# First layer's products at 164 columns, its gathered rows in four token sets, and the second layer's first gate computed in its own mixing

## The chip, the cores and the metric

The kernel runs on one core of one Trainium2 chip. The time is the device's, in microseconds, for one execution; the numbers below are medians of executions, and one further execution was profiled. TensorE (PE in the profile, its weight loads PEld) multiplies, VectorE (DVE) and ScalarE (ACT) work on elements, GpSimd (POOL) issues the indirect gathers, and SyncE (SP) issues most of the other transfers. The core has 16 DMA engines, which all queues share.

## The reference

One sequence of 256 tokens with 1024 features goes through two layers. Each layer is modulated by a conditioning vector `c`: six vectors of 1024 (shift, scale and gate for each of two halves) come out of one product with `w_ada`.

```python
def hybrid_layer(x, c_act, ...):
    mod = (c_act @ w_ada + b_ada)[:, None, :]
    sh1, sc1, g1, sh2, sc2, g2 = jnp.split(mod, 6, axis=-1)
    h = rms_norm(x, norm1_g) * (1 + sc1) + sh1
    proj = h @ w_in                       # attention, short convolution, spatial gating
    ...
    x = x + g1 * (merged @ w_out)
    h2 = rms_norm(x, norm2_g) * (1 + sc2) + sh2
    x = x + g2 * peer_ffn(h2, ...)

def peer_ffn(h, w_pq, sub_keys, expert_down, expert_up):
    # per token: 8 heads, each picks 16 of 128*128 experts by product keys
    ...
    u = expert_down[experts]              # 128 rows of 1024 for a token
    act = gelu(einsum('td,thkd->thk', t, u))
    wgt = gate * act
    vv = expert_up[experts]
    return einsum('thk,thkd->td', wgt, vv)
```

All is float32.

## The kernel before, in words

A layer has three stages. **Mixing**: 16 chunks of `w_in`, attention, convolution and gating, then 8 chunks of `w_out`. **Retrieval**: 16 chunks of `w_pq`, scores and the top-16 picks. **Experts**, by far the longest: the 16384 experts are taken in two ways at once.

- `T = DENSE[layer]` tokens (168 in the first layer, 160 in the second) are treated densely: all 16384 down vectors are multiplied with these tokens (128 chunks of 128 experts, 8 products each, `chunk_mm`, line 387; "down"), gelu and the gates are applied, and all up vectors are multiplied with the result (128 chunks, `add`, line 1201; "up"). The gates come as one-hot products for four tokens at a time (`compare`, `factors`, `gate_mm`, `gate_use`: VectorE, ScalarE, TensorE, then both again); there are `NG = T // 4` such groups.
- The other `TS = 256 - T` tokens (88 and 96) are treated by rows: for each of them GpSimd gathers the 128 down rows that it picked, one to a partition (`fetch`, line 1104), VectorE multiplies them with the token and sums (`dot`, line 1114); in up it gathers the 128 up rows, and VectorE adds them with their weights (`add_row`, line 1129 and, for the first of a set, 1127). These tokens are packed in sets of 64, 32, 16 or 8 (`token_sets`); each set has its copy of the tokens' inputs and its sum in one place of the tile `spots` (`R_DX`, `R_SUM`). At the end TensorE folds the sums of all sets into the result (`folds`, line 1207).

In `experts` the code of both halves stands in one order written by hand (`manual_schedule`), and each engine works through its instructions in that order. `dot` calls are spread over the chunks of down by a rate, `DOT_RATE`, per chunk; `add_row` calls evenly over chunks 4 to 124 of up. A row that has been used frees its buffer, and `fetch` issues the next gather. Buffers are places in the `arena` that are free at that time.

Weights are streamed in the order of the list `seq`, which the code builds for both layers. A chunk of kind "whole", "second" or "mat" goes through the ring `raw`, five units of two chunks; a "mat" chunk is then split in a high and a low part (`hi`, `lo`, three buffers each; ScalarE at line 297 or 299, VectorE at 290 or 292), so that TensorE can use three quicker products. Kind "ada" is a chunk of `w_ada`, and VectorE multiplies it with the activated `c` and sums (`ada_chunk`, line 243). Kind "aside" is the same for the next layer, loaded in the experts stage into the buffers of `hi` and `lo`, which are not used there, and worked off by `run_aside`, one at a time, in VectorE's order. `ASIDES_AT[layer]` says at which chunks of down the asides stand; the rest is spread over up. SyncE's queue takes these loads in order, and waits where a buffer is not free.

The first layer's experts carry 40 asides: the vectors 0 to 4 of the second layer. The second layer's experts carry 8 (vector 5).

## Time and profile before

| | |
|---|---|
| median of 3 runs | 1566.23 us (1564.98 to 1573.41) |
| profiled execution | 1569.29 us, span 1567.3 us |
| mean granted clock of TensorE | 0.991 |
| HBM read | 564.02 MB |
| first layer: down, up | about 190 to 513 us, 513 to 813 us |
| second layer: mixing and retrieval, down, up | 816 to 972 us, 972 to 1281 us, 1281 to 1560 us |

The page of the profile gives busy times of the engines, the span in 40 slices, the DMA queues, the chain of work that ended last, and groups of instructions with what ended the idle time before them (`<-`). A window is a stretch of the span, counted from its start. `x` is a count of instructions. TensorE handles one float32 product as two instructions, and in a busy stretch a matmul's recorded time overlaps the next one's, so the distance between them counts, not their length.

### The profile page before, as it was taken

The numbers are of one execution on the slowest core, as the hardware profiler recorded it, in microseconds if no ns is written. First come the engines' busy times: TensorE is split into PE (matmuls) and PEld (weight loads), VectorE is DVE, ScalarE is ACT, GpSimd is POOL, SyncE is SP. The second block draws the span as 40 slices with busy tenths as digits, with TensorE's granted clock in tenths as the row PEclk, the third lists the DMA queues.
The fourth block names the chain that finished last, engine by engine and source line by source line (L and its number), as shares of the span: only waits on it lengthen the run. The fifth ranks groups of instructions, "written<-read, shape, count | busy, mean of one in ns | idle before, by whom it ended". The sixth has DMA issues, their size and how long they took to land.

```text
span 1567.3 us, 28461 instructions
## 1 busy us (share of the span) xinstructions
PE 1537.3 (98%) x11240; PEld 1502.3 (96%) x11240; DVE 1000.1 (64%) x2255; ACT 475.9 (30%) x1356; POOL 496.1 (32%) x424
## 2 busy tenths in 40 slices
PE   7999999999999999999999999999999999999998
PEld 5879999999999999999999899999999999999998
DVE  6787897677787445544336678977777764444434
ACT  2346321465564000000025763224565620000000
POOL 1000133433443433434300001245354345445441
PEclk9999999999999999999999999999999999999999
DMA  9998289999999999999964562899999999999995
GB/s 385 366 383 296 98 318 339 419 422 421 422 420 415 418 423 422 423 424 422 424 243 161 188 245 97 322 350 423 423 423 421 419 420 423 423 423 422 423 424 245
DMA packets 121829, 571.16 MB, mean 364 GB/s; under 512 B 14259, under 2 KB 14787, under 8 KB 89568
## 3 DMA queue, kind: packets, MB, share of 16 engines
q1 hardware_dynamic: 48528, 241.06, 39.0%
q0 software_dynamic: 55744, 202.36, 32.2%
q10 hardware_dynamic: 17424, 125.93, 19.4%
q8 instruction: 88, 1.44, 0.3%
q14 instruction: 45, 0.37, 0.1%
HBM read 564.02 MB, written 4.09 MB: 362 GB/s over the span
## 4 chain that ended last, share of the span: by engine, by line
PE 80%; DMA 8%; issue 5%; POOL 3%; DVE 2%; ACT 1%; SPq 0%; POOLq 0%; DVEq 0%; ACTq 0%
PE acc L1201 37%; PE ch L387 26%; DMA arena<-in_down_rows,arena 6%; PE ch L389 2%; POOL arena L1104 2%; PE ch L390 2%; PE ch L391 2%; PE g L1163 1%; DMA raw<-in_w_ada 1%; PE ch L476 1%; PE acc L391 1%; PE g L982 1%; PE acc L389 1%; PE acc L390 1%; PE acc L387 1%
## 5 line engine op out<-in xcount | busy, mean ns | idle before, releaser
L1201 PE MATMUL acc<-arena,raw 128*128 128x168 f32 (+1 forms) x4096 | 575.3, 303 | 3.1 <-issue 3.1
L1201 PEld LDWEIGHTS acc<-arena,raw 128*128 128x128 f32 x4096 | 573.3, 191 | 3.5 <-issue 3.5
L387 PE MATMUL ch<-arena,raw 128*128 128x168 f32 (+2 forms) x3808 | 568.2, 308 | 1.6 <-issue 1.6
L387 PEld LDWEIGHTS ch<-arena,raw 128*128 128x128 f32 x3808 | 542.6, 191 | 8.0 <-issue 4.3
L1129 DVE SCALAR_TENSOR_TENSOR spots<-arena,spots 128x1024 f32<-128x1024 f32 x156 | 200.4, 1284 | 194.9 <-DMA arena<-in_up_rows,arena 193.6
L1104 POOL DMA_INDIRECT arena<-in_up_rows,arena x159 | 211.8, 1332 | 291.6 <-DMA arena<-in_up_rows,arena 172.0
L1104 POOL DMA_INDIRECT arena<-in_down_rows,arena x151 | 181.0, 1199 | 228.7 <-DVE arena L1114 169.9
L1114 DVE SCALAR_TENSOR_TENSOR arena<-arena,spots 128x1024 f32<-128x1024 f32 x151 | 182.9, 1222 | 59.9 <-DMA arena<-in_down_rows,arena 59.5
L243 DVE SCALAR_TENSOR_TENSOR aside<-aside,arena 128x1024 f32<-128x1024 f32 x48 | 58.6, 1221 | 69.2 <-DMA aside<-in_w_ada 69.2
L1147 ACT ACTIVATE arena<-arena,parts 128x128 f16<-128x128 f16 x164 | 64.6, 394 | 122.1 <-DVE arena L1137 102.7
L418 ACT ACT_TABLE_LOAD x6 | 7.7, 1283 | 275.5 <-PE acc L1201 275.4
L387 PE MATMUL ch<-arena 128*128 128x160 f32 (+2 forms) x512 | 81.5, 318 | 3.7 <-issue 1.9
L389 PE MATMUL ch<-hh,hi 128*128 128x256 f32 x288 | 82.6, 288 | 2.0 <-DVE arena L507 1.9
L387 PEld LDWEIGHTS ch<-arena 128*128 128x128 f32 x512 | 75.7, 193 | 8.4 <-ACT arena L440 4.1
L1180 ACT ACTIVATE arena<-ch 128x336 f32<-128x336 f32 (+32 forms) x122 | 42.2, 346 | 130.5 <-PE ch L387 101.7
L390 PE MATMUL ch<-hh,lo 128*128 128x256 f32 x288 | 81.8, 284 | 0.0
L391 PE MATMUL ch<-hh,hi 128*128 128x256 f32 x288 | 81.7, 284 | 0.0
L290 DVE TENSOR_TENSOR lo<-raw,hi 128x1024 fp32r<-128x1024 f32 x42 | 51.4, 1230 | 26.7 <-ACT hi L297 26.6
L1173 DVE SCALAR_TENSOR_TENSOR arena<-arena,g 128x336 f32<-128x336 f32 (+30 forms) x82 | 40.3, 492 | 43.9 <-ACT arena L1171 40.5
L243 DVE SCALAR_TENSOR_TENSOR raw<-raw,arena 128x1024 f32<-128x1024 f32 x48 | 58.4, 1225 | 8.6 <-DMA raw<-in_w_ada 5.1
L1151 ACT ACTIVATE arena<-arena,parts 128x128 f16<-128x128 f16 x164 | 63.4, 386 | 0.0
L1149 ACT ACTIVATE arena<-arena,parts 128x128 f16<-128x128 f16 x164 | 63.4, 386 | 0.0
(231 smaller groups left out, 1694.9 us busy)
## 6 DMA issues: line engine op xcount, KB each, us to landing
raw<-in_up SPq DMA_DIRECT2D x64, 1024.0 KB
raw<-in_up ACTq DMA_DIRECT2D x64, 1024.0 KB
raw<-in_down SPq DMA_DIRECT2D x58, 1024.0 KB
raw<-in_down ACTq DMA_DIRECT2D x56, 1024.0 KB
raw<-in_w_ada SPq DMA_DIRECT2D x48, 512.0 KB
aside<-in_w_ada SPq DMA_DIRECT2D x48, 512.0 KB
raw<-in_w_pq SPq DMA_DIRECT2D x32, 512.0 KB
arena<-in_down SPq DMA_DIRECT2D x28, 512.0 KB
```

What stands on the lines that cost most here:

```text
L243: nc.vector.scalar_tensor_tensor(raw, raw, 1.0, cact, op0=OP.mult, op1=OP.mult, accum_out=mods[layer][:, col:col + 1])
L387: nc.tensor.matmul(dst, hi[:, cols], k[0], start=start, stop=stop, **kw)
L389: nc.tensor.matmul(dst, hi[:, cols], k[0], start=start, stop=False, **kw)
L390: nc.tensor.matmul(dst, lo[:, cols], k[0], start=False, stop=False, **kw)
L391: nc.tensor.matmul(dst, hi[:, cols], k[1], start=False, stop=stop, **kw)
L1104: nc.gpsimd.indirect_dma_start(out=held[n], out_offset=None, in_=rows if n >= TS else down_rows[:, :], in_offset=bass.IndirectOffsetOnAxis ...
L1114: nc.vector.scalar_tensor_tensor(row, row, 1.0, R_DX[which(k)[0]], op0=OP.mult, op1=OP.mult, accum_out=R_DOTS[:, k:k + 1])
L1129: nc.vector.scalar_tensor_tensor(R_SUM[s], row, w, R_SUM[s], op0=OP.mult, op1=OP.add)
L1147: nc.scalar.activation(og[0][:, 0, i, :], oh[:, 0, i, :], AF.Copy, scale=parts[:, 0, t + i:t + i + 1])
L1149: nc.scalar.activation(og[1][:, 0, i, :], oh[:, 0, i, :], AF.Copy, scale=parts[:, 1, t + i:t + i + 1])
L1151: nc.scalar.activation(og[0][:, 1, i, :], oh[:, 1, i, :], AF.Copy, scale=parts[:, 0, t + 2 + i:t + 3 + i])
L1201: nc.tensor.matmul(acc[d // 2][:, (d % 2) * S:(d % 2) * S + T], u[:, d * P:(d + 1) * P], acts[:, i, :], start=i == 0 and d % 2 == 0, stop= ...
```

## The change

The dense part of the first layer goes from 168 to 164 tokens. Its rows are then 92, which need four sets (64, 16, 8, 4), so `token_sets` learns the size 4, all four places of `spots` hold sets, and the staging row `R_DROW` moves to a free place of the arena. `DOT_RATE` of the first layer goes from 0.85 to 0.88. Vector 2 of the second layer (`g1`, the gate of its first half) leaves the asides, 40 of which become 32, and its eight chunks are mixed as kind "ada" into the second layer's own list, between chunks 4 and 20 of `w_in` and `w_out`. The asides of both layers stand elsewhere. And two buffers, one of `hi` and one of `lo`, become row buffers for the length of `experts`.

```diff
-DENSE = (168, 160)
+DENSE = (164, 160)
...
-DOT_RATE = (0.85, 0.92)
+DOT_RATE = (0.88, 0.92)
...
-ASIDES_AT = ((20,) * 6 + tuple(range(46, 125, 5)), (20,) * 6 + (60, 72))
+ASIDES_AT = ((20,) * 4 + tuple(range(46, 116, 5)), (20,) * 4 + (50, 60, 70, 80))
 ASIDES_UP = (4, 100)
+MIXED = (4, 20)
...
 def token_sets(n):
-    for m in (64, 32, 16, 8):
+    for m in (64, 32, 16, 8, 4):
...
-    assert off == n and len(out) <= 3
+    assert off == n and len(out) <= 4
...
-        body += mix(tail[:6], ada(0, [5])) + tail[6:] if layer == 0 else tail
+        body = body + mix(tail[:6], ada(0, [5])) + tail[6:] if layer == 0 else mix(body + tail, ada(1, [2]), *MIXED)
...
-        aside = ada(1, [0, 1, 2, 3, 4] if layer + 1 < DEPTH else [5], "aside")
+        aside = ada(1, [0, 1, 3, 4] if layer + 1 < DEPTH else [5], "aside")
...
-        R_DROW = spots[:, 3, :]
         beyond = [region(at * S, D) for at in (80, 84) if at * S >= P * T]
+        R_DROW = spots[:, 3, :] if len(SETS) < 4 else beyond.pop()
         passing = []
-        free = deque([spots[:, n, :] for n in range(len(SETS), 3)] + [region(108 * S, D)] + beyond)
+        spare_rows = [stream.tile([P, D], F32, name="row", tag=tag, bufs=3) for tag in ("hi", "lo")]
+        free = deque([spots[:, n, :] for n in range(len(SETS), 3)] + [region(108 * S, D)] + beyond + spare_rows)
```

## The prediction

> **What bounds the kernel now.** I read the page's busy line and its GB/s row first, then the DMA issues, then stage by stage the windows, the chain of waits and single engines' timelines.

> ```profile
> span 1567.3 us, 28461 instructions
> ...
> PE 1537.3 (98%) x11240; PEld 1502.3 (96%) x11240; DVE 1000.1 (64%) x2255; ACT 475.9 (30%) x1356; POOL 496.1 (32%) x424
> ...
> GB/s 385 366 383 296 98 318 339 419 422 421 422 420 415 418 423 422 423 424 422 424 243 161 188 245 97 322 350 423 423 423 421 419 420 423 423 423 422 423 424 245
> ...
> aside<-in_w_ada SPq DMA_DIRECT2D x48, 512.0 KB
> ...
> spots<-dot_in POOLq DMA_DIRECT2D x3, 512.0 KB
> ```

> PE is busy for 98% of the span, which says TensorE. But the GB/s row is flat near 421 through both layers' expert stages (slices 8 to 20 belong to the first layer). Two resources are full at once, and the question is which of them has room left when the first layer ends. The windows of that layer (length, then busy time of PE, PEld, DVE, ACT, POOL, then granted clock, DMA share, GB/s):

> ```profile
> 235.00:255.00 20.00, 20.00 (x130) 20.00 (x130) 19.56 (x73) 3.67 (x7) 10.59 (x11) 0.91 0.92 268
> 255.00:275.00 20.00, 20.00 (x143) 20.00 (x142) 10.41 (x25) 4.11 (x10) 4.58 (x5) 1.00 1.02 416
> ...
> 285.00:513.00 228.00, 227.63 (x1770) 224.06 (x1769) 164.73 (x317) 126.62 (x449) 89.05 (x75) 1.00 1.02 420
> 513.00:660.00 147.00, 143.92 (x988) 143.47 (x987) 74.57 (x73) 0.29 (x1) 59.97 (x50) 0.98 1.02 421
> 660.00:790.00 130.00, 130.00 (x915) 130.00 (x914) 54.74 (x53) 1.28 (x1) 44.40 (x34) 1.00 1.02 423
> 790.00:800.00 10.00, 10.00 (x73) 10.00 (x72) 3.92 (x4) 0.29 (x1) 0.00 (x0) 1.00 0.82 293
> ```

> From 255 to 790 us the DMA moves 416 to 423 GB/s in these windows (268 before): it is full for 535 us, while PE is full too. Who gives way? In the second half of the layer ("up", 513 to 813) it is VectorE, in the groups of instructions of that stretch; the timelines of VectorE, TensorE and the SP queue at its end show by how much:

> ```profile
> L1129 DVE SCALAR_TENSOR_TENSOR spots<-arena,spots 128x1024 f32<-128x1024 f32 x76 | 97.6, 1284 | 73.2 <-DMA arena<-in_up_rows,arena 72.2
> ...
> 796.42 1.28 DVE L1129 SCALAR_TENSOR_TENSOR spots<-arena,spots 128x1024 f32<-128x1024 f32 x1 [1.16 <-DMA arena<-in_up_rows,arena]
> ...
> 810.09 0.73 PE L1207 MATMUL acc<-fold,spots 128*128 128x64 f32 x6
> ...
> 792.90 34.36 SPq L229 DMA_DIRECT2D raw<-in_w_in  x14
> ```

> VectorE stands 73.2 us before row additions, 72.2 of it for the rows' gathers. The last row is added at 797.7 us, and it still waited 1.16 us for its gather. TensorE needs the sums first in its folds (L1207), at 810.1 us. So the DMA side has 12.4 us of room at the end of the first layer, and this is all of it. The next layer's weights (in_w_in) start at 792.9, when the rows are nearly through.

> **The change part by part.**

> *Products 164 wide.* Per chunk eight products, each recorded as two instructions, so 32 instructions for a pair of chunks. The chain of waits in the first layer and in the second, which is already 160 wide:

> ```profile
> 430.08 4.62 PE ch L387 x32
> 434.70 0.46 PE g L1163 x8
> 435.16 4.61 PE ch L387 x32
> ...
> 1139.04 4.40 PE ch L387 x32
> 1143.44 0.46 PE g L1163 x8
> 1143.90 4.40 PE ch L387 x32
> ```

> A pair takes 5.08 us with its gate at 168 columns and 4.86 at 160: 0.22 us for eight columns, 0.11 for four. Times 64 pairs that is 7.0 us in each of the two halves, 14.0 us. One gate group of four tokens fewer (42 to 41): 0.46 us. TensorE would so be 14.5 us earlier at the fold: 795.6 us.

> *Four more row tokens, eight fewer side weights.* A row gather and a side weight (aside) are both 128x1024 f32, 512 KB, one block of 0.524 MB; at 421 GB/s a block costs 1.245 us of DMA. Each half gets four row gathers more (88 to 92) and four asides fewer (22 to 18 in down, 18 to 14 in up): no change in bytes. But the time in which they must move is shorter. In the steady part of down a pair needs two weight chunks, 2 x 0.85 rows and 0.4 asides, 4.10 blocks or 5.10 us, against a pair of 5.08: in balance. Afterwards it is 2 + 1.76 + 0.4 = 4.16 blocks, 5.18 us, against 4.97 on TensorE. Chunks 46 to 111 are 32 pairs: rows come up to 6.8 us late there. VectorE takes its work in order, so the gates' factors queue behind a late row's dot product, and TensorE waits for them. Two further row buffers (one, net, in this layer, since the fourth set takes a place) hold rows; they do not move bytes. I expect 0 to 6.8 us of waits in down, say 3; it won't matter for the sum, because of what comes next.

> The two buffers come out of the tags hi and lo, which the asides use: they have four places in place of six. An aside without a place holds the SP queue, and half of the chunks' weights stand behind it there. From the waits of the SP queue:

> ```profile
> SPq L229 <- DVE aside L243: 25.9, 4, 12.9
> ```

> Up to 12.9 us, four times, and TensorE did not wait. As asides in the list fall by as much (four at chunk 20 for four places), I cost it at nothing; without that cover it is one such wait less what the weights are ahead, at most 12.9 us.

> *The end of the first layer.* What must land before the last row: one copy more of the inputs for the fourth set (the dot_in issues go from 3 to 4), one block; two asides fewer loaded ahead of 255 us (the list starts with four at chunk 20, was six), two blocks that move into the full stretch; less one block for the added buffer. Net two blocks, 2.5 us. And next-layer weights: they follow TensorE's release of buffers, 14 issues in 34.36 us, so 7 in the 17.2 us from 792.9 to the fold. With TensorE ahead, those 7 blocks start ahead of the last rows and share the DMA: 8.7 us. Against it the window 790 to 800 had 128 GB/s unused, up to 3 us. Bounds: the last addition at 797.7 (nothing pushed) to 809 (all pushed); nearest is all pushed, as the queue is full to the end: 807 us. TensorE, ready at 795.6 or a little later, waits some 11 us at its fold for what it won. The fold starts 3 us earlier than before, not 14.5.

> *Folds of a fourth set.* 8 column blocks, two instructions each, 16 more. The chain has:

> ```profile
> 813.12 3.45 PE acc L1207 x30
> ```

> 0.115 us each, 1.8 us on the path. *The clock after the wait.* A stop of TensorE has a price, seen where up begins:

> ```profile
> 522.00:528.00 6.00, 2.92 (x15) 2.47 (x14) 4.13 (x5) 0.00 (x0) 3.00 (x5) 0.82 1.03 425
> 528.00:534.00 6.00, 6.00 (x28) 6.00 (x27) 0.00 (x0) 0.00 (x0) 1.68 (x2) 0.61 1.04 429
> ```

> 3.1 us idle, then granted clocks of 0.82 and 0.61 over 12 us: 3.4 us of work lost. At the fold I take 2.5, between nothing and 3.4, since VectorE's updates take part of the path there. [...]

> Down and up of the first layer together: -3 + 1.8 + 2.5 = +1.3 us.

> *Second layer's first gate in its own mixing.* Eight weights of 512 KB now come in the main ring on SP, between chunks 5 and 19 of that layer, each followed on VectorE by one multiply-and-sum, and one addition at the end. Prices and places:

> ```profile
> L243 DVE SCALAR_TENSOR_TENSOR raw<-raw,arena 128x1024 f32<-128x1024 f32 x48 | 58.4, 1225 | 8.6 <-DMA raw<-in_w_ada 5.1 <-ACT arena L445 3.5
> ...
> 107.00:114.00 7.00, 5.28 (x33) 4.44 (x31) 4.30 (x8) 3.43 (x6) 0.00 (x0) 0.92 0.99 380
> 114.00:121.00 7.00, 5.98 (x32) 5.98 (x33) 5.17 (x9) 1.28 (x2) 0.00 (x0) 0.59 1.02 419
> 850.00:874.00 24.00, 24.00 (x193) 22.99 (x192) 21.25 (x55) 17.56 (x52) 0.00 (x0) 1.00 0.49 161
> 874.00:890.00 16.00, 16.00 (x114) 11.64 (x113) 6.98 (x12) 10.46 (x19) 0.61 (x1) 1.00 0.26 90
> ```

> The DMA has room there (161 and 90 GB/s). VectorE: 8 x 1.225 = 9.8 us in some 70; from 874 on it is idle for half the time, but from 850 to 874 it has 2.75 us free and would get three or four of the eight, 3.7 to 4.9 us. What queues behind are the low halves of the weights and the softmax steps, for which TensorE waits. Bounds: 0 (all in gaps) to 9.8. The nearest row is the first layer's output stage, which already carries eight such weights: TensorE idle 1.72 + 1.02 us from 107 to 121, with its DMA full, which here it isn't. I take 2.

> *Second layer's experts.* Asides at chunks 20 (four) and 50 to 80, instead of six and two; two more row buffers. A pair needs 2 + 1.84 blocks, 4.78 us, of 4.86: enough for two asides over 40 pairs. 0, between -2 and +2.

> Sum: +1.3 + 2 + 0 = +3.3 us. The profiled execution took 1569.29 us (span 1567.3), 3.06 above the median of 1566.23; on the median the sum gives 1569.5.

> **Rivals.** *A, the DMA does not end last.* For it: TensorE has never waited for weights (98% busy), and the rows' margin of 12.4 us is close to the 14.5 us that TensorE gains; if the rows end by 796, the whole gain stays: 1566.2 - 14.5 + 1.8 + 2 = 1555.5. It needs 11 us of DMA time from somewhere, and no window shows more than 429 GB/s in 6 us or 423 in 130. [...] The trace bears 421.

> *B, slower: VectorE in the second layer's mixing.* One place, 850 to 874 us: if the eight multiply-and-sums delay the low halves one for one, TensorE loses up to 9.8 us: 1566.2 + 1.3 + 9.8 = 1577.3. It decides once the weights' lead over TensorE is used up, that is when more than 2.75 us land in that window. For it: VectorE at 89% there. Against it: its 56% free right behind.

> *C, the layer ends as before.* The forecast is in part this: the columns saved do not show, as the rows' bytes set the end. How far it is complete is the 797.7 to 809 above.

> **How the numbers follow.** What can be told from no change is about 0.5%, 7.8 us. Forecast with C: 0.56, 1564 to 1576 (rows' end 803 to 812, mixing 0 to 5). A: 0.22, 1550 to 1561. B: 0.22, 1575 to 1584. Faster than 1558.4: A's share, 0.22; slower than 1574: B and the forecast's upper edge, 0.24; same 0.54. The range leaves out A's lower part and B's upper part, a tenth each: 1555 to 1579.

> **What would show it.** Right: pairs 4.97 us apart in down where nothing waits; the GB/s row still flat, and longer, to the layer's end; a wait of TensorE of about 10 us at L1207 or at the products before it, released by L1129; in_w_in issues ahead of the last row addition; the layer's end within 4 us of 816.6 (813.12 + 3.45); eight L243 instructions among L290 in the mixing. Wrong: no wait at L1207 and the layer ended by 806 (A), or idle TensorE in the mixing, released by L290, L517 or L721, of over 5 us (B). A wait of TensorE in down of more than 7 us would show the gates queued behind late rows to be worse than I have it.

## The result, and the profile after

The changed kernel took 1584.97 us in the median of five runs (1584.09 to 1586.43), the kernel before 1566.23 (now 1563.33 to 1573.41 in five): a ratio of 1.0113, 95% interval 1.0092 to 1.0134. It is slower, by more than the range (up to 1579) allowed for. Of the changed kernel's page, the busy line, the GB/s row and the costliest row of VectorE:

```profile
span 1584.7 us, 28490 instructions
...
PE 1533.9 (97%) x11248; PEld 1495.4 (94%) x11248; DVE 1005.7 (63%) x2267; ACT 471.4 (30%) x1347; POOL 526.2 (33%) x435
...
GB/s 385 360 388 298 102 300 353 422 422 422 421 421 410 422 423 422 423 424 422 422 175 204 218 244 96 303 342 411 423 421 422 421 422 424 423 423 422 423 424 232
...
L1131 DVE SCALAR_TENSOR_TENSOR spots<-arena,spots 128x1024 f32<-128x1024 f32 x137 | 176.1, 1286 | 228.5 <-DMA arena<-in_up_rows,arena 226.8
```

TensorE is busy for 3.4 us less (1537.3 before), and the span is 17.4 us longer: time went into stops, not into work. The GB/s row stands near 422 from slice 8 to slice 20 (410 in slice 13), as it did before; that the DMA is full for longer shows in the window from 790 to 800 us below, with 420 GB/s where the kernel before had 293. (L1131 is the row addition, L1129 before.) Where the stages begin in the two traces, in us, and how much longer each one became:

| stage | before | after | change | forecast |
|---|---|---|---|---|
| first layer's down | 190.1 to 512.6 | 189.8 to 514.0 | +1.7 | -4.5 |
| its up, to the first fold | to 810.1 | to 798.6 | -12.8 | -7.0 |
| first fold to the second layer's start | to 816.4 | to 824.5 | +19.6 | +12.8 |
| second layer's mixing | to 914.7 | to 927.8 | +5.0 | +2 |
| retrieval | to 971.3 | to 984.4 | 0 | 0 |
| second layer's down | to 1280.6 | to 1297.9 | +4.3 | 0 |
| up and the end | to 1567.3 | to 1584.7 | +0.1 | 0 |

(Forecast: 7.0 us for each half, 0.46 for the gate group and 3 of waits in down; the third row is what its +1.3 leaves. The first row starts 0.3 us earlier in the changed kernel.) Up gained more than its 7.0, as the stop at 522 to 534 us is gone. The windows of the changed kernel's first layer, columns as in the forecast's windows:

```profile
285.00:513.00 228.00, 222.29 (x1722) 215.29 (x1721) 163.04 (x313) 122.99 (x438) 91.33 (x77) 0.99 1.02 419
513.00:660.00 147.00, 146.66 (x1055) 146.55 (x1054) 68.43 (x64) 0.44 (x1) 61.48 (x47) 1.00 1.02 423
660.00:790.00 130.00, 130.00 (x936) 130.00 (x935) 53.46 (x51) 1.58 (x2) 52.96 (x38) 1.00 1.02 423
790.00:800.00 10.00, 9.15 (x68) 9.05 (x66) 5.26 (x4) 2.09 (x2) 2.13 (x4) 1.00 1.03 420
800.00:810.00 10.00, 0.59 (x2) 0.50 (x2) 5.45 (x5) 0.20 (x1) 0.00 (x0) 0.57 0.56 229
810.00:825.00 15.00, 14.51 (x65) 14.51 (x66) 6.83 (x14) 4.30 (x11) 0.00 (x0) 0.50 0.20 71
```

In down TensorE is now idle for 5.7 us of 228. From 800 to 810 it does nothing, as the forecast has it. But then it does its folds for 14.5 us at a granted clock of 0.50. The timelines of TensorE and of VectorE at that place:

```profile
798.64 0.51 PE L1209 MATMUL acc<-fold,spots 128*128 128x64 f32 x4
801.64 0.59 PE L1209 MATMUL acc<-fold,spots 128*128 128x8 f32 x2 [2.49 <-DVE spots L1131]
810.49 0.59 PE L1209 MATMUL acc<-fold,spots 128*128 128x4 f32 x2 [8.26 <-DVE qg L566]
...
816.14 8.53 PE L1209 MATMUL acc<-fold,spots 128*128 128x64 f32 x40
```

```profile
807.83 1.28 DVE L1131 SCALAR_TENSOR_TENSOR spots<-row,arena,spots 128x1024 f32<-128x1024 f32 x1 [1.25 <-DMA row<-in_up_rows,arena]
809.15 1.28 DVE L1131 SCALAR_TENSOR_TENSOR spots<-arena,spots 128x1024 f32<-128x1024 f32 x1
810.35 0.15 DVE L566 TENSOR_SCALAR qg<-vec 128x1 f32<-128x1 f32 x1
```

The fold needs the fourth set last, and the last addition ends at 810.4. (The 8.26 us are put down to L566, the small instruction that follows it on VectorE.) The 40 fold instructions at the end take 0.21 us each; in the kernel before a fold instruction took 0.115. The trace's record of the granted clock has it at half (a granted clock of 0.50) from 801.3 us for 27.3 us without a break.

### The profile page after: what moved, and what is told of

It reads as the page before. It is cut to its first block, busy times and chain, and to the rows that moved or that the text cites. A ratio compares the mean times of both kernels' runs of the same rounds, so it can differ in the third digit from the quotient of the medians.

```text
span 1584.7 us, 28490 instructions
## 1 busy us (share of the span) xinstructions
PE 1533.9 (97%) x11248; PEld 1495.4 (94%) x11248; DVE 1005.7 (63%) x2267; ACT 471.4 (30%) x1347; POOL 526.2 (33%) x435
## 3 DMA queue, kind: packets, MB, share of 16 engines
HBM read 568.74 MB, written 4.11 MB: 361 GB/s over the span
## 4 chain that ended last, share of the span: by engine, by line
PE 49%; DMA 32%; issue 7%; DVE 6%; POOL 4%; ACT 2%; SPq 0%; POOLq 0%; ACTq 0%; DVEq 0%
PE acc L1203 18%; PE ch L388 17%; DMA arena<-in_up_rows,arena 15%; DMA arena<-in_down_rows,arena 7%; DMA row<-in_up_rows,arena 3%; POOL arena L1106 3%; DMA raw<-in_w_ada 2%; PE ch L390 1%; PE ch L391 1%; PE ch L392 1%; DMA row<-in_down_rows,arena 1%; DMA spots<-in_down_rows,arena 1%; PE ch L477 1%; PE g L1165 1%; PE acc L392 1%
## 5 line engine op out<-in xcount | busy, mean ns | idle before, releaser
L1203 PE MATMUL acc<-arena,raw 128*128 128x164 f32 (+1 forms) x4096 | 566.3, 301 | 0.3 <-issue 0.3
L388 PE MATMUL ch<-arena,raw 128*128 128x164 f32 (+2 forms) x3808 | 561.5, 306 | 5.1 <-ACT arena L1185 3.5
L1131 DVE SCALAR_TENSOR_TENSOR spots<-arena,spots 128x1024 f32<-128x1024 f32 x137 | 176.1, 1286 | 228.5 <-DMA arena<-in_up_rows,arena 226.8
L1116 DVE SCALAR_TENSOR_TENSOR arena<-arena,spots 128x1024 f32<-128x1024 f32 x129 | 156.4, 1222 | 68.0 <-DMA arena<-in_down_rows,arena 67.7
L1149 ACT ACTIVATE arena<-arena,parts 128x128 f16<-128x128 f16 x162 | 63.8, 394 | 138.4 <-DVE arena L1139 130.8
L1182 ACT ACTIVATE arena<-ch 128x320 f32<-128x320 f32 (+40 forms) x122 | 41.8, 342 | 125.2 <-PE ch L388 101.9
L244 DVE SCALAR_TENSOR_TENSOR raw<-raw,arena 128x1024 f32<-128x1024 f32 x56 | 67.7, 1216 | 14.3 <-DMA raw<-in_w_ada 10.5
L1131 DVE SCALAR_TENSOR_TENSOR spots<-row,arena,spots 128x1024 f32<-128x1024 f32 x32 | 41.1, 1285 | 54.7 <-DMA row<-in_up_rows,arena 54.6
L1106 POOL DMA_INDIRECT row<-in_down_rows,arena x42 | 51.0, 1214 | 60.5 <-DVE row L1116 30.7
L1165 PE MATMUL g<-arena 128*128 128x128 f16 x648 | 59.3, 220 | 6.7 <-ACT arena L1149 5.2
L1175 DVE SCALAR_TENSOR_TENSOR arena<-arena,g 128x176 f32<-128x176 f32 (+20 forms) x81 | 39.8, 492 | 38.7 <-ACT arena L1173 37.9
L1153 ACT ACTIVATE arena<-arena,parts 128x128 f16<-128x128 f16 x162 | 62.6, 386 | 0.0
## 6 DMA issues: line engine op xcount, KB each, us to landing
raw<-in_w_ada SPq DMA_DIRECT2D x56, 512.0 KB
aside<-in_w_ada SPq DMA_DIRECT2D x40, 512.0 KB
raw<-in_w_pq SPq DMA_DIRECT2D x32, 512.0 KB
arena<-in_down SPq DMA_DIRECT2D x28, 512.0 KB
```

The lines of the kernel that those rows point to most:

```text
L244: nc.vector.scalar_tensor_tensor(raw, raw, 1.0, cact, op0=OP.mult, op1=OP.mult, accum_out=mods[layer][:, col:col + 1])
L388: nc.tensor.matmul(dst, hi[:, cols], k[0], start=start, stop=stop, **kw)
L1106: nc.gpsimd.indirect_dma_start(out=held[n], out_offset=None, in_=rows if n >= TS else down_rows[:, :], in_offset=bass.IndirectOffsetOnAxis ...
L1116: nc.vector.scalar_tensor_tensor(row, row, 1.0, R_DX[which(k)[0]], op0=OP.mult, op1=OP.mult, accum_out=R_DOTS[:, k:k + 1])
L1131: nc.vector.scalar_tensor_tensor(R_SUM[s], row, w, R_SUM[s], op0=OP.mult, op1=OP.add)
L1149: nc.scalar.activation(og[0][:, 0, i, :], oh[:, 0, i, :], AF.Copy, scale=parts[:, 0, t + i:t + i + 1])
```

## The experiments

The theory: the bytes of the rows set the first layer's end, TensorE's wait for them costs the clock, and the mixing and the second layer's down each have a stop of their own. Each measured ratio below is to the kernel before on the same chip, with its 95% interval.

**1. Fewer bytes ahead of the last row.**

```diff
+                if Src.loaded in Src.short:      # the side weights in up of layer 0
+                    raw, src = raw[:, :64], src[:, :64]
...
-        nc.vector.scalar_tensor_tensor(raw, raw, 1.0, cact, ...
+        nc.vector.scalar_tensor_tensor(raw, raw, 1.0, cact[:, :raw.shape[1]], ...
```

> The changed kernel with the side weights in up of the first layer loaded, multiplied and summed on 64 of their 1024 columns (this leaves out most of two of the second layer's modulation vectors). About 13 of 14 blocks of 1.245 us, some 16 us of DMA, are gone from the last 300 us of that layer; the rows, the columns, the four sets and the order stay. Theory (the bytes set when the last row is added, and the 27 us at half clock follow from TensorE's wait for it): last row addition at 795 to 800 us (810.4 in the changed kernel), TensorE waits under 3 us at its first fold (11.9), no half clock of over 7 us there, folds in 6 to 8 us (14.1), second layer starts at 804 to 808 (824.5), total 1565 to 1570. Rival (rows late through their own latency, their buffers or the order of VectorE's work, not bytes): last addition after 806, total above 1578. A second rival (the clock falls for the load of the stage, whatever TensorE waits for): half clock of over 20 us near 800 all the same, folds over 12 us.

Measured: ratio 1.0011 (0.9985 to 1.0038), median 1569.27 us. The last addition came at 780.6, 30 us earlier where 10 to 15 were expected, TensorE did not wait at the fold, and the second layer began at 809.3 (804 to 808 expected). Beside the 16 us of bytes that are gone, the next layer's weights, issued from 780.4 us on, now come too late to share the DMA with the rows. The edit also makes the side weights' sums on VectorE short, but VectorE still waits 127.9 us for rows between 513 and 782 us, so it was not its time that the rows lacked. The bytes do set the end of the rows. But the clock fell all the same, for 13.7 us from 800.5. Its TensorE timeline and its windows there:

```profile
797.20 0.95 PE L1214 MATMUL acc<-fold,spots 128*128 128x64 f32 x8
...
800.95 8.54 PE L1214 MATMUL acc<-fold,spots 128*128 128x64 f32 x40
```

```profile
797.20:800.50 3.30, 3.30 (x31) 3.30 (x30) 2.11 (x4) 0.62 (x2) 0.00 (x0) 0.99 0.24 92
800.50:809.30 8.80, 8.80 (x42) 8.80 (x43) 2.89 (x6) 3.68 (x10) 0.00 (x0) 0.50 0.35 119
```

TensorE has no idle time in either window, and in the second its clock is half. The folds took 12.3 us from first to last. So the theory was right on the bytes and wrong on the clock, where the second rival holds half: the wait makes the half clock longer (27.3 us against 13.7) but does not begin it alone.

**2. The next layer's weights held back.**

```diff
+            if Src.loaded == Src.hold and Src.last_row:   # SP, ahead of the next layer's first weight
+                nc.sync.dma_start(hold_dram, Src.last_row.pop()[:, 0:1])
...
```

> The changed kernel, but the next layer's first weights (in_w_in) are issued only once the first layer's last gathered row has landed: SP first issues a 512-byte transfer that reads that row. Nothing is left out. Theory (seven of these blocks share the DMA with the last rows, 8.7 us): last row addition 6 to 9 us earlier, at 801 to 804 (810.4); TensorE's wait at the first fold 3 to 6 us (11.9); second layer's start 4 to 15 us earlier than 824.5, by how much of the half clock goes; what the held weights cost at the second layer's start 0 to 3 us; total 1572 to 1582. Rival (the rows' gathers end last for another reason and the weights only use what is free): last addition within 2 us of 810, total 1584 to 1590.

Measured: ratio 1.0092 (1.0063 to 1.0121), median 1581.75 us. VectorE's last addition, and TensorE at the next layer's start:

```profile
799.22 1.28 DVE L1140 SCALAR_TENSOR_TENSOR spots<-arena,spots 128x1024 f32<-128x1024 f32 x1
```

```profile
821.57 4.65 PE L484 MATMUL ch<-arena,raw 128*128 128x257 f32 x10 [9.04 <-ACT arena L490]
```

The addition ends at 800.5, 9.9 us earlier (6 to 9 expected): the blocks that share the DMA with the last rows are the term that the forecast has at 8.7. But the held weights are then late themselves, and 9.04 us are lost at the start of the second layer, where I had expected 0 to 3. It started 3.0 us earlier, less than the 4 to 15 expected, and half clock still lasted 23.9 us: the wait was moved, not removed.

**3. TensorE kept at work while it waits.**

```diff
+ if i == 127 and d == FOLD_LAG and layer == 0:
+     warm = bank("ch", 2)                                     # a spare bank
+     for n in range(48):
+         nc.tensor.matmul(warm[:, :T], ..., acts[:, i, :], start=True, stop=True)
```

> The changed kernel, and TensorE does 48 further products (96 instructions of 128 rows by 41 columns) of the last chunk into an unused bank between its last products and its first fold in the first layer, about 10 us of work in the place of its wait of 11.9 us. Nothing is left out. Theory (the wait brings the clock down, and the folds run at half clock for that): last row addition unchanged at 810 +-1.5, half clock of under 8 us between 798 and 830 (27.3), folds in 6.3 to 9 us (14.1), second layer starts 5 to 8 us earlier than 824.5, total 1576 to 1580. Rival (the folds are slow because VectorE's updates between them pace them): folds still 13 to 15 us, total 1584 to 1587.

Measured: ratio 1.0106 (1.0074 to 1.0137), median 1583.99 us. The timeline of TensorE (the added products are 164 columns wide, not 41 as the expectation says):

```profile
795.81 11.85 PE L1234 MATMUL ch<-arena,raw 128*128 128x164 f32 x84
807.50 1.24 PE L1209 MATMUL acc<-fold,spots 128*128 128x64 f32 x8
...
811.49 8.53 PE L1209 MATMUL acc<-fold,spots 128*128 128x64 f32 x40
```

The last addition came at 808.3, and the second layer began 4.7 us earlier (5 to 8 expected). The folds came straight out of wide products at full clock and still took 12.5 us, with half clock from 811.1 for 13.7 us. Neither side had it: VectorE does not pace them (nothing waits between the 40), and the wait is not what slows them here.

**4. The first gate in its own mixing, alone on the kernel before.**

```diff
- ASIDES_AT = ((20,) * 6 + tuple(range(46, 125, 5)), (20,) * 6 + (60, 72))
+ ASIDES_AT = ((20,) * 4 + tuple(range(46, 116, 5)), (20,) * 6 + (60, 72))
+ MIXED = (4, 20)
...
- body += mix(tail[:6], ada(0, [5])) + tail[6:] if layer == 0 else tail
+ body = body + mix(tail[:6], ada(0, [5])) + tail[6:] if layer == 0 else mix(body + tail, ada(1, [2]), *MIXED)
...
- aside = ada(1, [0, 1, 2, 3, 4] if layer + 1 < DEPTH else [5], "aside")
+ aside = ada(1, [0, 1, 3, 4] if layer + 1 < DEPTH else [5], "aside")
```

> The kernel before (168 columns, three sets, its row buffers and its second layer as they were) with only this part of the change: the second layer's first gate is computed in its own mixing, and 8 side weights fewer are loaded in the first layer (four at chunk 20, then 14 from chunk 46). Theory (part by part): the mixing of the second layer takes 103 us as in the changed kernel (98.3 before), +4 to +6; the first layer's TensorE gains nothing from the bytes, as it did not wait for them, second layer's start 814 to 817 (816.4); second layer's down 309 (309.2, against 313.5 in the changed kernel, which so belongs to its buffers or its aside places); total 1569 to 1573. Rival (the mixing is 5 us longer because the first layer ended with a long half clock and its weights came late behind the rows): mixing within 1.5 us of 98.3, total 1564 to 1568.

Measured: ratio 1.0013 (0.9987 to 1.0039), median 1567.66 us. The mixing took 103.4 us, so its 5 us come from this part and not from the first layer's end. Second layer's down: 308.9, as in the kernel before. What I had not expected: with eight side weights fewer the first layer ended 8.3 us earlier (808.1): 3.0 us in down and 4.7 in up, where the stop at 522 to 534 is gone. The kernel before was already short of DMA there.

**5. Sixteen thin products more, on the kernel before.**

```diff
  # after the three sets of each block d
+ if layer == 0:
+     nc.tensor.matmul(thin[:, :4], R_SUM[0][:, d * P:(d + 1) * P], fold[layer][:, 0:4], ...)
...
```

> The kernel before (three sets, 168 columns, no wait at the fold) with 16 products more among the first layer's folds: two instructions of 4 columns behind each block's three sets, of the shape that a fourth set has, into a spare bank. Nothing is left out. Theory (a long run of narrow products is too little work for the clock: from 64 instructions on it falls while the folds still run): the folds take 11 to 14 us (6.3 in the kernel before), half clock for over 10 us from 811 to 816 on, the second layer starts 5 to 8 us later than 816.4, total 1571 to 1576. Rival (each instruction has its 0.115 us and no more; the long half clock comes from TensorE's wait, or from the next layer's start): folds 8.1 us, half clock at most 6.8 us, second layer +2, total 1567 to 1570.

Measured: ratio 1.0018 (1.0001 to 1.0036), median 1572.26 us against 1568.40. Folds 9.9 us (6.5 from first start to last end in the kernel before), half clock from 815.0 for 6.8 us, second layer 2.5 us later. That lies between the two expectations: 3.4 us, 1.8 for the instructions and 1.6 for the clock. A fold of 64 instructions of the same widths cost 12.3 in experiment 1; when the clock fell differs, 3.3 us behind the first fold there and 5.9 here (see the last section).

**6. The same folds, wide.**

```diff
  # wide: for the sets of 16, 8 and 4, the fold's columns among zeros, 92 columns in all
+ if layer == 0 and s:
+     nc.tensor.matmul(acc[d // 2][:, at - off:at - off + TS], R_SUM[s][...], wide[:, s - 1], ...)
+     continue
  nc.tensor.matmul(acc[d // 2][:, at:at + n], R_SUM[s][...], fold[layer][:, off:off + n], ...)
...
```

> The kernel with the side weights in up of the first layer cut to 64 columns (as in the first experiment, and so with the same part left out), and the folds of the sets of 16, 8 and 4 tokens made 92 columns wide by zero columns: the same 64 instructions and the same sums. Theory (the clock falls because the narrow products leave the array idle): the folds take 7 to 8.5 us (12.1 in the first experiment), no half clock, or at most 3.4 us, between 797 and 812, second layer starts 3.5 to 5 us earlier than 809.3, total 1563 to 1567. Rival (the clock falls at the change from products to folds for another reason, such as their weight loads, whatever the columns): folds over 11 us, half clock again 13.7 us, total 1568 to 1571.

Measured: ratio 0.9983 (0.9961 to 1.0005), median 1565.14 us (1569.27 in experiment 1, on another chip). Its windows, to be held against those of experiment 1:

```profile
799.80:803.20 3.40, 3.40 (x31) 3.40 (x30) 2.11 (x4) 0.60 (x2) 0.00 (x0) 1.00 0.24 94
803.20:807.90 4.70, 4.70 (x44) 4.70 (x43) 1.75 (x4) 3.36 (x10) 0.00 (x0) 1.00 0.66 219
```

The same 64 fold instructions, nearly four times the columns, no half clock, and 8.1 us in the place of 12.3. The folds differ in their columns alone, so in these two runs, where TensorE did not wait, it was the small number of columns streamed that brought the clock down (0.50 there, 1.00 here), and not the instructions or their weight loads. The second layer began at 807.8, only 1.5 us earlier (3.5 to 5 expected), since TensorE reached the fold 2.6 us later (799.85).

**7. The gate's weights early in the mixing.** As experiment 4, with

```diff
- MIXED = (4, 20)
+ MIXED = (4, 12)
```

> The kernel before with only the first gate in its own mixing, but the eight weights come between chunks 4 and 12 of that stage and not between 4 and 20; in this form ScalarE's instructions there stand in the order of the kernel before. Nothing is left out. Theory (the mixing's +5 us comes from ScalarE's order: a table load of 1.28 us ahead of a copy that TensorE waits for, 2.4 to 2.7 us, with 3.4 us at half clock behind it): mixing 98 to 100 us (103.4 with 4 to 20), no half clock in it, second layer's down 309, second layer's start 808 to 816, total 1556 to 1563. Rival (the eight multiply-and-sums of 1.23 us on VectorE are the price wherever they stand): mixing 102 to 105, a half clock in it, total 1563 to 1568.

Measured: ratio 0.9994 (0.9980 to 1.0008), median 1565.74 us (1556 to 1563 expected); mixing 100.4 us, without the half clock that experiment 4 has from 873.0 us. The waits of TensorE in the mixing of experiment 4, and then ScalarE's timeline in the kernel before, in experiment 4 and in this one:

```profile
PE acc L676 <- ACT arena L666: 2.7, 1, 2.7
```

```profile
872.82 1.05 ACT L665 COPY arena<-acc 128x512 f32<-128x512 f32 x2
873.89 1.28 ACT L405 ACT_TABLE_LOAD   x1
```

```profile
870.06 0.57 ACT L666 COPY arena<-acc 128x512 f32<-128x512 f32 x1
870.66 1.28 ACT L406 ACT_TABLE_LOAD   x1
...
872.16 0.56 ACT L666 COPY arena<-acc 128x512 f32<-128x512 f32 x1
```

```profile
866.68 1.06 ACT L666 COPY arena<-acc 128x512 f32<-128x512 f32 x2
867.75 1.28 ACT L406 ACT_TABLE_LOAD   x1
```

With the weights from 4 to 20 the table load stands between two copies, and TensorE waits 2.7 us for the second; its clock is half for 3.4 us behind that. With 4 to 12 the copies stay together, and 3 of the 5 us are gone. The 8 x 1.23 us on VectorE are the same in both. The other 2 us stay, and 1.7 of them are two short stops of TensorE between 821 and 826 us, both for VectorE. First the waits, then VectorE's timeline ahead of the first of them:

```profile
PE ch L390 <- DVE arena L508: 0.9, 1, 0.9
PE acc L392 <- DVE hh L518: 0.8, 1, 0.8
```

```profile
820.46 1.22 DVE L244 SCALAR_TENSOR_TENSOR raw<-raw,arena 128x1024 f32<-128x1024 f32 x1
...
821.60 1.67 DVE L518 SCALAR_TENSOR_TENSOR hh<-arena,mod,hh 128x256 fp32r<-128x256 f32 x4
```

An added multiply-and-sum (L244) stands ahead of the instructions that TensorE waits for. So the rival holds for this smaller part.

**8. No spare row buffers in the second layer.**

```diff
- free = deque([...] + [region(108 * S, D)] + beyond + spare_rows)
+ free = deque([...] + [region(108 * S, D)] + beyond + (spare_rows if layer == 0 else []))
...
```

> The changed kernel without the two spare row buffers in the second layer; they stay in the first, and the side weights keep their places. Nothing is left out. Theory (two more row buffers let more gathers run at once and hold up the weights at the start of the second layer's down): second layer's down 308.5 to 310 us (313.5 in the changed kernel), the first layer unchanged within 2 us, total 1580 to 1582. Rival (the aside places, four at chunk 20 and four from 50 to 80, cost the 4.3 us): down still 312.5 to 314.5, total 1584 to 1586. A second rival (the rows now come later for want of buffers): over 315.

Measured: ratio 1.0091 (1.0063 to 1.0118), median 1582.40 us; second layer's down 310.9 us. One profile says little on 2.6 us, but those of all the kernels can be put together: with the spare buffers and the new aside places 312.1 to 313.6 (seven profiles, mean 312.8), without the buffers 310.9 and 311.8 (this and experiment 12), with the arrangement of before 308.9 to 311.3 (five, mean 310.2). So some 1.4 of 2.6 us go with the buffers, on two profiles against seven; the rest goes with the aside places or is scatter. The stretch that differs most, 76 to 130 us into down, in the kernel before, in the changed one and in this one:

```profile
1047.35:1101.35 54.00, 52.57 (x397) 51.49 (x397) 35.57 (x66) 23.77 (x80) 25.30 (x20) 0.97 1.02 422
```

```profile
1060.42:1114.42 54.00, 49.78 (x371) 48.66 (x370) 34.24 (x65) 21.08 (x72) 28.65 (x20) 0.97 1.01 414
```

```profile
1058.67:1112.67 54.00, 50.08 (x377) 48.99 (x376) 34.96 (x66) 22.85 (x78) 26.05 (x20) 0.97 1.01 413
```

TensorE stands 2.8 us longer there in the changed kernel, with the DMA full, and without the spare buffers it stands almost as long: this stop is not theirs. Over all profiles TensorE stands 3.9 to 7.2 us in this stretch with the new aside places (nine), and with the old ones (five) 0.3 to 2.0, but once 5.5 (experiment 9). That points to the places and does not show them to be the cause. TensorE's waits over the changed kernel's down of that layer name ScalarE's gelu for 3.5 us and a chunk's weights for 0.8 us:

```profile
PE ch L388 <- ACT arena L1185: 3.5, 1, 3.5
PE ch L388 <- issue: 1.5, 3, 0.7
PE ch L388 <- DMA raw<-in_down: 0.8, 1, 0.8
```

**9. Early gate weights and wide folds, on the kernel before**, the edits of 6 (88 columns) and 7.

> The kernel before with the first gate between chunks 4 and 12 of its own mixing, and with the folds of the first layer's sets of 16 and 8 tokens made 88 columns wide by zero columns: 48 instructions as before. Nothing is left out; it is meant as the version that could beat both kernels. Theory (narrow folds bring the clock down at the end of the first layer, 3.4 us at half from 808.3, half of it lost): no half clock between 800 and 815, folds 5.4 to 6.3 us, 1 to 2 us off the whole, total 1561 to 1565 (1565.7 with the narrow folds). Rival (three sets are few enough, the half clock there comes from the next layer's start): half clock again near 808, total 1565 to 1567.

Measured: ratio 1.0007 (0.9990 to 1.0023), median 1564.12 us against 1564.32. The half clock between 800 and 815 is gone, as expected, but the folds took 6.3 us as in experiment 7, and the whole did not move. Its first layer's down took 323.6 us, against 319.6 in experiment 7, although the edits leave that part alone; such scatter hides 1 to 2 us. No version that computes everything beat the kernel before.

**10. All side weights of the first layer short**, the edit of experiment 1 in down too.

> The changed kernel with all side weights of the first layer, in down and in up, loaded and summed on 64 of 1024 columns (this leaves out most of five of the second layer's modulation vectors). Theory (the rows are late in down because the DMA is full: 4.16 blocks for each pair of chunks, 0.4 of them side weights): down 315 to 319 us (324.2 in the changed kernel, 324.8 where only up was relieved), so that the 164 columns show; second layer's start 800 to 806, total 1558 to 1565. Rival (what stalls TensorE in down is the order of work on VectorE and ScalarE: dot products issued at a higher rate, gates behind them): down 322 to 325 all the same, total 1565 to 1570.

Measured: ratio 0.9963 (0.9944 to 0.9982), median 1558.34 us. Down took 314.9 us, 9.3 less than in the changed kernel: with the DMA relieved, the 164 columns show their 7 us. The stretch from 255 to 504 us, first of the changed kernel and then of this one:

```profile
255.00:504.00 249.00, 243.29 (x1873) 236.29 (x1872) 177.84 (x343) 130.39 (x462) 101.55 (x85) 0.99 1.02 419
```

```profile
255.00:504.00 249.00, 245.81 (x1924) 242.92 (x1923) 162.92 (x349) 133.88 (x465) 110.88 (x90) 0.99 1.01 405
```

There are 2.5 us more of PE busy time, on 51 matmuls more, and 14.9 us less of DVE, at 405 GB/s. So the edit takes work from VectorE too; but from 285 to 504 us VectorE waits for rows for 10.1 us here and for 40.3 in the changed kernel, so it was rows that it lacked and not time. The second layer began at 798.5 (800 to 806 expected).

**11. The dot products' rate as before.**

```diff
- DOT_RATE = (0.88, 0.92)
+ DOT_RATE = (0.85, 0.92)
```

> The changed kernel with the rate of dot products in the first layer's down at 0.85 for each chunk as before, not 0.88; the products that don't come there come in up. Nothing is left out. Theory (VectorE reaches dot products whose rows haven't landed; at the lower rate it stands less): down 319 to 322 us (324.2), but the same bytes have to come, so the last row addition stays at 808 to 812 and the total within 2 us of the changed kernel, 1582 to 1586. Rival (the rate is no part of it, the bytes are): down 323.5 to 326.

Measured: ratio 1.0152 (1.0127 to 1.0177), median 1586.76 us. Down took 319.0 us, 5.2 less than in the changed kernel's profile, and nothing came of it: the last addition ended at 808.7, and TensorE, at its fold at 793.2, waited for it longer:

```profile
PE acc L1209 <- DVE spots L1131: 9.7, 1, 9.7
PE acc L1209 <- DVE qg L566: 4.8, 1, 4.8
```

How much of the 5.2 us is the rate's is not shown: seven profiles with the changed kernel's down lie between 320.5 us (experiment 3) and 325.5, and VectorE's waits for rows from 285 to 504 us are no shorter (40.7 us, against 40.3). What the shorter downs of experiments 3 and 11 do show is that they don't move the layer's end; only the bytes and their order do.

**12. Three parts mended together in the changed kernel**: the edits of 6, 7 and 8.

> The changed kernel with three parts mended together: the gate's weights between chunks 4 and 12 of the mixing, the small sets' folds 92 columns wide, no spare row buffers in the second layer. Nothing is left out. Theory (the parts add up: mixing -3, folds -3 to -6 by the clock, second layer's down -2.6): last row addition still 808 to 812, folds behind it 8 to 11 us (14.1), mixing 99 to 101 (103.3), down 310 to 312 (313.5), total 1572 to 1577; what is left over the kernel before is the first layer's rows, 6 to 11 us. Rival (the half clock after TensorE's wait of 11.9 us lasts whatever the folds are): folds 13 us or more, total above 1578.

Measured: ratio 1.0079 (1.0055 to 1.0103), median 1576.29 us; last addition 811.4, mixing 99.9, down 311.8. The windows at the fold:

```profile
799.00:812.00 13.00, 1.70 (x9) 1.30 (x8) 7.81 (x8) 0.20 (x1) 0.00 (x0) 0.61 0.58 236
812.00:821.00 9.00, 9.00 (x64) 9.00 (x64) 5.40 (x11) 4.07 (x11) 0.00 (x0) 0.80 0.36 118
```

Behind TensorE's wait the clock now recovers within the folds (mean 0.80 against 0.50), and they take 9.4 us from the last addition, not 14.1. The parts add up (some 4.7 us at the folds, 3.4 in the mixing and 1.7 in down, less 0.9 for a later last addition): 9 us of the span. Of the other 8.2 us, the second layer's start at 820.8 holds 4.4.

## Why the prediction was wrong, step by step

The traces differ by +17.4 us, the sum said +3.3. The 14.1 us between them are four terms that were mis-sized, and behind one of them, the clock, stands a step that was wrong in kind.

- *Products 164 wide*: right. A pair is 4.51 + 0.46 = 4.97 us in the chain of waits after, as forecast:

```profile
433.36 4.51 PE ch L388 x32
437.86 0.46 PE g L1165 x8
```

- *Waits in down*: I took 3 of at most 6.8 us (32 pairs of 0.21 us are 6.7), and TensorE's down came out 6.2 us longer than by that, 9.2 in all. The stalls were worse than my bound: from 285 to 513 us TensorE's weight loads stood still for 12.7 us, against 3.9 before. That it "won't matter for the sum" was right: down was 5.2 us shorter in experiment 11 and 3.7 in experiment 3, and the last addition stayed.
- *The end of the rows*: 807 forecast, bound 809, measured 810.4 (808.3 to 811.4 in the five kernels with the same bytes). **+3.4 us**. The mechanism was right (experiments 1, 2 and 10); the next layer's weights cost 9.9 rather than 8.7. That is the price of eight blocks of 1.245 us, where I had counted seven (an estimate: SP issues the six below, then one of the mixed gate at 795.2 and another of `in_w_in` at 795.6). With it the bound of 809 becomes 810.2; the 2 us that I took off for unused bandwidth were not there. Their issue ahead of the rows, in the SP queue's timeline:

```profile
781.85 9.71 SPq L230 DMA_DIRECT2D raw<-in_w_in  x6
```

- *The clock after the wait*: this is the step that failed in kind. I had folds and clock at 6.3 + 1.8 + 2.5 = 10.6 us and the bounds of the clock at 0 to 3.4; it was 14.1, **+3.5 us**. I priced a wait followed by full work, from 522 to 534 us. But what follows here is 64 products of 64, 16, 8 and 4 columns, in which the clock did not come back (0.50 from 810 to 825 us) and, without any wait ahead of them, fell to 0.50 (experiments 1, 3 and 5; at 92 columns, in experiment 6, it stayed at 1.00). With wide columns the clock came back within the folds (a mean of 0.80 in experiment 12).
- *The mixing*: 2 taken, of 0 to 9.8; 5.0 measured, **+3.0 us**. In the changed kernel TensorE waits 2.4 us for ScalarE's second copy, half clock for 3.4 us behind it costs 1.7, and 0.9 are waits for VectorE: 5.0 together. So the greater part is not VectorE's 8 multiply-and-sums themselves (rival B) but that the added weights moved the order of ScalarE's instructions (experiment 7). Rival B holds for the 0.9, near the start of the stage and not from 850 to 874 us. I had looked for the queue behind the added work on the engine that does it, and not at the order on the other.
- *Second layer's experts*: 0 (-2 to +2) taken, **+4.3 us** measured between these two profiles, 2.6 between the means of experiment 8. I had costed the two further row buffers and the new aside places as free, on a mean of 4.78 us of DMA in 4.86. Some 1.4 us go with the buffers. The stop in the stretch where the DMA is full, at 414 GB/s, early in down, stays without them, and its cause is open.

Rival A's premise can now be seen by itself. With the rows in time (experiment 1) the kernel took 1569.3 us and not 1555.5: of the 12.9 us by which TensorE was earlier at the fold, 5.8 went into its folds, 5.8 into the mixing and 3.1 into the second layer's down. So its price was wrong too, by the same terms. Rival C was the right centre: the saved columns did not show, since the bytes set the end.

## What to carry to other kernels

When two resources are full and the change relieves only the one, price the end of the other, and then what the engine that waits does *next*: a tail of narrow products paid twice here (14.1 us behind the wait, 9.4 with wide columns). Count columns, not busy time, to see whether TensorE keeps its clock (busy without a stop in experiments 1 and 6, granted 0.50 and 1.00); zero columns up to a width of 92 cost these folds no time (a group of eight fold and two wide instructions took 1.17 us in experiment 6 as in experiment 1). An added instruction in a scheduled stage may cost nothing on its own engine and yet reorder another (experiment 4: a table load of 1.28 us between two copies, 2.7 us on TensorE): compare the order of every queue.

## What the runs showed of the hardware

The half-clock stretches of the kernel before begin at 112.9, 235.7, 525.9, 816.0 and 1082.2 us and last 6.83, 3.41, 6.83, 3.41 and 3.41 us (a sixth, from 1563.5, ends with the kernel). In this trace their starts are 36, 85, 85 and 78 times 3.413 us apart, the length of the shorter ones. What folds of the same widths cost went with when the clock fell: 12.3 and 12.5 us where it fell 3.3 and 3.6 us behind the start of the first of them (experiments 1 and 3), 9.9 where it fell 5.9 us behind it (experiment 5).
